# A hybrid decoder layer: TensorE's order from the recurrence to the second norm taken from a table, attention's half of the output projection first, latents left unscaled

## The chip, the cores and the metric

The kernel runs on one core of a Trainium2 chip. The metric is the device time of one execution in microseconds (us). A core has five engines with their own queues: TensorE (PE; its weight loads are PEld), VectorE (DVE), ScalarE (ACT), GpSimd (POOL) and SyncE (SP), which issues most DMAs. TensorE writes to PSUM, here eight banks of 128 x 512 floats; the other working memory is SBUF.

## The reference

One decoder layer on 256 tokens of width 2048, in float32:

```
h = rms_norm(x, attn_norm_g);  proj = h @ w_in
h_r, h_k, h_v, h_w, h_a, h_g = split(token_shift(proj[:, :3360]))
c_q, c_kv, k_pe = split(proj[:, 3360:])              # 512, 512, 64 columns
y_rwkv = (group_norm(rwkv7_scan(r, decay, k, v, -kk, kk * a)) + bonus) * g    # 16 heads x 64
q  = rms_norm(c_q)  @ w_uq;   kv = rms_norm(c_kv) @ w_ukv                     # the "latents"
y_mla = softmax((q_nope k_nope + rope(q_pe) rope(k_pe)) / sqrt(192)) v        # 8 heads, causal
x = x + concat(y_rwkv, y_mla) @ w_out
h = rms_norm(x, ffn_norm_g)                          # the second norm
x = x + (silu(conv3(h @ w_gate)) * (h @ w_up)) @ w_down
out = rms_norm(x, final_norm_g)
```

`rwkv7_scan` keeps a 64 x 64 state per head and updates it for every token: `state = state * w + (state a) b + v k`, output `state r`.

## The kernel before, in words

Every large weight comes as a *piece* of 128 x 1024 floats (512 KB). `piece` (L130) issues its DMA on SP's queue, casts it to a rounded `hi` on ScalarE (L138) and takes the rest `lo = raw - hi` on VectorE (L139). A product then is three matmuls: hi by hi, hi by lo, lo by hi. `raw`, `hi` and `lo` have three buffers each, so about three pieces can be ready ahead of TensorE. PSUM is divided into three banks `mm` (large products), three `ch` and two `at` (all small things).

The input projection runs tile by tile (`in_tile`, L226: two pieces, 48 matmuls). Keys come first, then receptance, then values. The recurrence is done in four chunks of 64 tokens and two halves of heads (`hf`). Its *factors* are built beside the projection: Gram matrices `G1`, the transposed `BKt`, and a triangular inverse. The inverse is found by `solve` (L612) on VectorE, 31 steps of two instructions, for 32 x 32 corners; the result goes through DRAM and comes back as `TT` and `T11` in another layout (L626 to L640). The remaining corners are 32 x 32 matmuls (`pR`, `pT`, L674 and L686), each followed by copies to `RT` and `TT`.

`chunk` (L705) is the recurrence: for each half a row product from local values and the state (`px`), the solved rows (`px` again, through `TT`), the output (`py`) from state and local values, and the state's update `ST`. Each is 8 small matmuls (16 instructions in the profile, L717), and each hands over to the next through VectorE or ScalarE copies (L743, L751, L760, L761, L767).

`latent` (L820) makes the two latents from input tiles 27 to 34: scaled by the first norm's `rsB` into `cr` (L826), squared and summed, split into `cl`, and their own root `rr` found on GpSimd by `rsqrt` (L233). `spread` (L858) turns `rr` into a row factor `rrB` by a matmul with ones (L262). `up_b` (L862) makes queries and keys (12 matmuls for each of two outputs) and multiplies each result by `rrB` on VectorE; L893 makes attention's values `vm`. `scores` (L906) and `attend` (L930) do one head. `group_norm` (L781) norms the recurrence's output for one half of the tokens, gates it (L803, L804) and transposes it into `yhi`/`ylo` (L808 to L812). The output projection (L968) has two halves: rows of the RWKV heads first, then rows of the attention heads. Behind the second, each 512-column tile of the new `x1` is transposed (L991) into `zs` for the feed-forward part, and the second norm's root is taken.

The order: the kernel is written in program order, and a scheduler that simulates a timeline orders each engine's instructions by readiness and program order. Before the change that also holds for TensorE in the stage that matters here; only `issue_after` binds some pairs. A block `manual_schedule(engines=...)` fixes the order in which an engine takes the instructions traced inside it.

## Time and profile before

| | |
|---|---|
| median of 3 runs (lowest to highest) | 1191.44 us (1190.81 to 1192.54) |
| the profiled execution | 1188.67 us |
| its span, first to last instruction | 1186.9 us |
| mean granted TensorE clock | 0.989 |
| TensorE busy | 1164.7 us (98%) |
| VectorE busy | 805.5 us (68%) |
| ScalarE busy | 603.9 us (51%) |
| bytes moved by DMA | 215.98 MB, mean 182 GB/s |

"Busy" is the union of instruction times. Matmuls are pipelined: one instruction's modelled end lies behind the start of the next, so the distance between starts tells what a matmul costs, and a busy TensorE can still be waiting or slow. The granted clock is 1.00 at full speed. A wait is idle time of an engine before an instruction, put down to what ended it. A row of the timeline begins with start and length in us, then engine, line, operation, result and operands, shapes and count.

### The profile page before, as it was taken

To read this page: it belongs to the slowest core of one execution; us is meant where nothing else is said; L and a number is where in the kernel's file an instruction comes from. 1 tells how busy PE (TensorE), PEld (TensorE's weight loads), DVE (VectorE), ACT (ScalarE), POOL (GpSimd) and SP (SyncE) were. 2 spreads that over 40 slices of the span, in tenths; PEclk is the share of its full clock that TensorE was granted. 3 is DMA by queue.
4 is the path that set the end of the run, shared out by engine and by line. 5 is a ranking of instruction groups with operands and counts; after the bars stand their busy time and mean duration, and the time that the engine had idled before them with its cause. 6 is when DMAs were issued, how large, how long until landed. Compare 5 with 4: busy or idle time off the path is not lost.

```text
span 1186.9 us, 19485 instructions
## 1 busy us (share of the span) xinstructions
PE 1164.7 (98%) x7673; PEld 1024.5 (86%) x7673; DVE 805.5 (68%) x1301; ACT 603.9 (51%) x894; POOL 29.4 (2%) x86
## 2 busy tenths in 40 slices
PE   9999999998989999999999999999999999999996
PEld 9899999997858888888888888888888888888885
DVE  7897669644975566777777775444577777775563
ACT  7874345433425456655555554333455555554441
POOL 1200000003000001000000000000000000000000
PEclk9999999998999999999999999999999999999998
DMA  9645456714425555656556566565555555566671
GB/s 335 196 148 162 134 169 195 220 53 127 160 89 171 161 184 176 197 194 195 193 184 194 192 195 192 193 190 192 195 194 194 195 189 189 194 228 212 199 227 71
DMA packets 71131, 215.98 MB, mean 182 GB/s; under 512 B 17616, under 2 KB 18000, under 8 KB 71040
## 3 DMA queue, kind: packets, MB, share of 16 engines
q1 hardware_dynamic: 69920, 211.97, 55.4%
q10 hardware_dynamic: 768, 2.05, 0.6%
q8 instruction: 60, 0.98, 0.3%
q0 software_dynamic: 352, 0.72, 0.2%
q14 instruction: 31, 0.25, 0.1%
HBM read 210.58 MB, written 3.41 MB: 180 GB/s over the span
## 4 chain that ended last, share of the span: by engine, by line
PE 92%; DVE 4%; DMA 1%; ACT 1%; issue 1%; POOL 1%; SPq 0%; ACTq 0%; DVEq 0%; POOLq 0%
PE mm L177 27%; PE mm L183 14%; PE mm L196 11%; PE mm L219 9%; PE mm L220 9%; PE mm L221 9%; PE mm L199 5%; PE pg L568 1%; PE px L717 1%; PE py L717 1%; DVE lo L139 1%; PE at L196 1%; PE wps L330 1%; DMA Lp<-dL 1%; DMA qs<-qr 0%
## 5 line engine op out<-in xcount | busy, mean ns | idle before, releaser
L139 DVE TENSOR_TENSOR lo<-raw,hi 128x1024 fp32r<-128x1024 f32 x376 | 460.0, 1224 | 269.7 <-ACT hi L138 202.7
L138 ACT CAST hi<-raw 128x1024 fp32r<-128x1024 f32 x376 | 395.5, 1053 | 421.5 <-PE mm L221 139.7
L177 PE MATMUL mm<-z,hi 128*128 128x512 f32 x1408 | 351.9, 392 | 0.0
L177 PEld LDWEIGHTS mm<-z,hi 128*128 128x128 f32 x1408 | 251.5, 188 | 43.0
L183 PEld LDWEIGHTS mm<-z,lo 128*128 128x128 f32 x1408 | 186.5, 188 | 14.9
L183 PE MATMUL mm<-z,lo 128*128 128x256 f32 x1408 | 189.3, 277 | 0.0
L196 PE MATMUL mm<-x,hi 128*128 128x256 f32 x1024 | 138.7, 284 | 0.0
L220 PE MATMUL mm<-lo,hh 128*128 128x512 f32 x336 | 130.7, 389 | 0.0
L221 PE MATMUL mm<-hi,hl 128*128 128x512 f32 x336 | 130.7, 389 | 0.0
L196 PEld LDWEIGHTS mm<-x,hi 128*128 128x128 f32 x1024 | 126.1, 190 | 2.1 <-issue 0.3
L219 PE MATMUL mm<-hi,hh 128*128 128x512 f32 x336 | 119.7, 389 | 0.0
L221 PEld LDWEIGHTS mm<-hi,hl 128*128 128x128 f32 x336 | 63.0, 188 | 13.2
L199 PE MATMUL mm<-x,lo 128*128 128x256 f32 x512 | 74.3, 283 | 0.0
L219 PEld LDWEIGHTS mm<-hi,hh 128*128 128x128 f32 x336 | 63.1, 188 | 13.0
L220 PEld LDWEIGHTS mm<-lo,hh 128*128 128x128 f32 x336 | 63.1, 188 | 13.0
L199 PEld LDWEIGHTS mm<-x,lo 128*128 128x128 f32 x512 | 65.8, 191 | 1.6 <-issue 1.3
L220 PE MATMUL mm<-lo,yhi 128*128 128x512 f32 x128 | 52.2, 408 | 0.0
L221 PE MATMUL mm<-hi,ylo 128*128 128x512 f32 x128 | 50.7, 397 | 0.0
L219 PE MATMUL mm<-hi,yhi 128*128 128x512 f32 x128 | 49.8, 406 | 0.3 <-ACT yhi L811 0.3
L219 PEld LDWEIGHTS mm<-hi,yhi 128*128 128x128 f32 x128 | 24.4, 192 | 7.1 <-issue 1.5
L196 PE MATMUL mm<-cl,hi 128*128 128x256 f32 x160 | 25.6, 306 | 4.8 <-DVE qr L209 2.0
L221 PEld LDWEIGHTS mm<-hi,ylo 128*128 128x128 f32 x128 | 24.5, 191 | 5.8 <-DVE bv L775 0.8
(279 smaller groups left out, 1057.1 us busy)
## 6 DMA issues: line engine op xcount, KB each, us to landing
raw<-in_wgu SPq DMA_DIRECT2D x176, 512.0 KB, 3.3
raw<-in_wdn SPq DMA_DIRECT2D x88, 512.0 KB, 4.2
raw<-in_win SPq DMA_DIRECT2D x70, 512.0 KB, 4.0
raw<-in_wout SPq DMA_DIRECT2D x32, 512.0 KB, 3.4
raw<-in_wuq SPq DMA_DIRECT2D x6, 512.0 KB, 4.4
xraw<-in_xT SPq DMA_DIRECT2D x4, 512.0 KB, 6.2
xt<-in_x SPq DMA_DIRECT2D x4, 512.0 KB, 6.8
raw<-in_wuv SPq DMA_DIRECT2D x4, 512.0 KB, 3.4
```

What stands on the lines that cost most here:

```text
L138: S.copy(hi, raw)
L139: last_lo[0] = V.tensor_tensor(lo, raw, hi.bitcast(F32), ALU.subtract).ins
L177: PE.matmul(accs[i], pcs[p][0][:, j * P:(j + 1) * P], act(h * 8 + j), start=h == 0 and j == 0, stop=False, skip_group_check=True)
L183: PE.matmul(accs[i][:, :T], lo[:, j * P:(j + 1) * P], act(h * 8 + j)[:, 0, :], start=False, stop=h == 1 and j == 7, skip_group_check=True)
L196: PE.matmul(acc[:, :T], hi[:, j * P:(j + 1) * P], act(kt0 + j)[:, s, :], start=first and j == 0 and s == 0, stop=False)
L199: i = PE.matmul(acc[:, :T], lo[:, j * P:(j + 1) * P], act(kt0 + j)[:, 0, :], start=False, stop=last and j == n - 1)
L219: PE.matmul(accs[tb], ah, wh, start=first and j == 0, stop=False)
L220: PE.matmul(accs[tb], ah, wl, start=False, stop=False)
L221: i = PE.matmul(accs[tb], al, wh, start=False, stop=last and j == n - 1)
L330: PE.matmul(wps[:, :P], ones, ones, start=True, stop=True)
L568: PE.matmul(pg[h][:, o:o + P], BK[pp][hs, gg, w * 2 + r, :, :], AR[pp][hs, gg, w * 2 + r, :, :], start=o == 0, stop=True, skip_group_check ...
L717: ins.append(PE.matmul(dst[HS[h], a_ * 64:(a_ + 1) * 64], lhsT, rhs, start=begin and n == 0 and a_ == 0, stop=True, skip_group_check=True) ...
```

## The change

From the corner matmuls to the transposes of `x1`, TensorE's instructions are written as short steps and put in one order by two strings, inside `manual_schedule(engines={PE})`. `STREAM` lists the large products (`l` latent tiles, `q` rope queries, `Q`/`K` queries and keys, `v` values, `W` output projection). They are generators that stop after 8 matmuls (256 columns) or 4 (512 columns): a latent tile has 6 steps, `q`, `Q`, `K` 3 each, `v` 6, `W` 12, 186 in all. `PLAN` is read from left to right: a number takes so many steps of the stream, a letter does one small unit.

- The latent tiles begin as before, while the solve runs; the corners `R` come after 32 steps, and most of chunks 0 to 2 between steps 34 and 38 of the stream.
- The latents are not multiplied by `rsB` any more: `cl` and the squares are taken straight from PSUM, and the first norm's root `rs1` (kept by one more GpSimd copy) enters the latents' roots, which now are taken on VectorE.
- Queries are not multiplied by `rrB` but copied by ScalarE; the factor `rrs[0]` goes into the maximum and the scale of the exponential. `spread` for the queries falls away. Keys and values are scaled as before.
- Heads are scored in the order 0, 2, 1, 3, 4, ..., with the transposes of the probabilities (`P`) and the products with the values (`A`) as separate units.
- The output projection takes attention's rows first (`W1..`), then the RWKV rows (`W0..`, tiles 0, 2, 1, 3). The group norms `N`, the gates `G` and the transposes `Y` lie beside the attention half. `x1` is transposed (`X`) near the end.
- The gate's loads wait for chunk 3's output copies instead of chunk 1's.

```
+        rs1 = con([P, 2], "rs1")
+        nc.gpsimd.tensor_copy(rs1, rsqrt(ssx[:, 0:2], 1.0 / DM, EPS, 2))
+        bcast(rs1, rsB)
...
+    def solved(c, hf):
+        pu = px_.pop((c, hf))[:, 256:512]
+        pairs(c, hf, pu, lambda p, a_, h: (TT[HS[h], c * 8 + p, :], XB[hf][HS[h], a_ * 64:(a_ + 1) * 64]), True)
+        for h in range(2):
+            (S.copy if h else V.tensor_copy)(UV[c][64:128, hf * 4:hf * 4 + 4, HS[h]],
+                                             pu[HS[h]].rearrange("p (a v) -> p a v", a=4))
...
+    def latent_tile(x, j):
...
+        h_, l_ = (c_[j // 2][:, j % 2, q, :] for q in range(2))
+        S.activation(h_, acc, AF.Copy, scale=vv(gname, j))
+        V.scalar_tensor_tensor(l_, acc, vv(gname, j), h_.bitcast(F32), ALU.mult, ALU.subtract)
+        sq = t2("csq") if j else ssum
+        S.activation(sq, acc, AF.Square)
+        if j:
+            V.tensor_tensor(ssum, ssum, sq, ALU.add)
...
+    def latent_root(x):
...
+        V.tensor_tensor(m, pss[:, 0:4:2], rs1, ALU.mult)
+        V.tensor_tensor(m, m, rs1, ALU.mult)
+        V.scalar_tensor_tensor(rrs[x], rsqrt(m, 1.0 / 512, EPS, 2, V), (SC, 1.0)[x], rs1, ALU.mult, ALU.mult)
...
+    def evict():
+        while waiting and (True and waiting[0][0] == 0 or waiting[0][0] in rrB):
+            x, dsts, accs = waiting.pop(0)
+            for j in range(2):
+                if True and x == 0:
+                    S.copy(dsts[j], accs[j][:, :T])
+                else:
+                    scaled(dsts[j], accs[j], rrB[x])
...
+    def gate_loads():
+        gnwb.extend([s4(n=n) for n in ("gnw", "gnb")])
+        with tc.issue_after(ylast[3]):
...
-            S.activation(pe_[:, ks], psc[:, ks], AF.Exp, bias=mx[:, qb:qb + 1], accum_out=sm[:, qb:qb + 1])
+            V.tensor_tensor(mx[:, qb:qb + 1], mx[:, qb:qb + 1], rrs[0][:, qb:qb + 1], ALU.mult)
+            S.activation(pe_[:, ks], psc[:, ks], AF.Exp, bias=mx[:, qb:qb + 1], scale=rrs[0][:, qb:qb + 1],
+                         accum_out=sm[:, qb:qb + 1])
...
+    small = {
+        "R": corner_r, "T": corner_t, "w": rows, "x": rows_state, "i": solved, "s": out_state, "u": update,
+        "o": out_local, "r": latent_root, "b": spread, "c": swap, "e": rope, "g": gate_loads, "S": scores,
+        "P": turn_p, "A": attend, "N": norm, "G": gated, "Y": turn_y, "X": turn_x,
+    }
+    STREAM = """
+    l00 l01 l02 l03 l10 l11 l12 l13 q0 q1 v0 K0 Q0 K1 Q1 v1 K2 Q2 Q3 K3 W100 W110 W120 W130 W001 W021
+    W011 W031
+    """.split()
+    PLAN = """
+    25 w00 3 r0 4 R0 R1 2 T0 w01 1 i00 i01 u00 w11 u01 w10 o01 T1 x10 x11 o00 s10 i10 i11 s11 u10 u11
+    w20 w21 o10 o11 x20 x21 s20 i20 i21 1 u20 s21 w30 1 u21 1 w31 o21 x31 x30 2 i31 1 s31 o20 1 o31 i30
+    g s30 3 o30 7 r1 5 c 3 b1 6 e 3 S0 3 S2 1 S1 1 P0 S3 1 P1 1 A0 4 P3 1 A1 3 N0 A3 1 P2 1 S4 1 S5 A2 3
+    S6 2 P4 1 P5 1 A5 2 A4 S7 1 P6 A6 2 P7 A7 4 N1 12 G00 1 G01 1 G10 Y01 16 G11 1 Y10 2 Y00 7 Y11 37
+    X10 1 X00 X01 X21 3 X11 1 X20 1 X30 X31
+    """.split()
+    with tc.manual_schedule(engines={mybir.EngineType.PE}):
+        big = stream()
+        for s in PLAN:
+            if s.isdigit():
+                for _ in range(int(s)):
+                    next(big, None)
+            else:
+                small[s[0]](*map(int, s[1:]))
+        for _ in big:
+            pass
```

## The prediction, made before the changed kernel was run

> **What bounds the kernel now.** The profile's page comes first: how long the profiled execution is, and what each weight piece costs VectorE.

> ```profile
> span 1186.9 us, 19485 instructions
> ...
> L139 DVE TENSOR_TENSOR lo<-raw,hi 128x1024 fp32r<-128x1024 f32 x376 | 460.0, 1224 | 269.7 <-ACT hi L138 202.7
> ```

> This execution took 1188.67 us (its span and 1.8 us around it); the three timed runs have a median of 1191.44 us. I sum against the profile and apply the difference to the median. The page says that TensorE is nearly always busy, but the change touches one stage, from the first latent tile to the second norm. So the second view is the table of stretches, cut at that stage's seams. Its columns are the length, busy time (instructions) of TensorE, its weight loads, VectorE, ScalarE and GpSimd, the granted TensorE clock, the DMA share and GB/s.

> ```profile
> core 0: us, PE busy (x) PEld busy (x) DVE busy (x) ACT busy (x) POOL busy (x), PEclk, DMA share, GB/s
> 194.20:228.60 34.40, 34.40 (x303) 34.28 (x301) 29.12 (x56) 18.40 (x27) 0.00 (x0) 1.00 0.71 206
> 231.90:235.20 3.30, 3.30 (x16) 3.30 (x17) 1.54 (x2) 1.89 (x3) 0.00 (x0) 0.50 0.97 374
> 254.70:261.40 6.70, 6.70 (x191) 6.25 (x190) 2.97 (x8) 1.89 (x6) 0.00 (x0) 1.00 0.23 81
> 276.40:279.70 3.30, 3.30 (x17) 3.30 (x17) 2.06 (x4) 1.76 (x3) 2.72 (x8) 0.51 0.40 92
> 283.50:290.10 6.60, 6.39 (x21) 5.59 (x22) 4.31 (x11) 1.04 (x1) 3.87 (x10) 0.52 0.53 130
> 290.10:346.30 56.20, 54.31 (x335) 45.19 (x333) 48.76 (x102) 22.97 (x40) 0.00 (x0) 1.00 0.46 145
> 351.30:358.10 6.80, 6.80 (x13) 3.40 (x12) 1.38 (x2) 1.15 (x2) 0.00 (x0) 0.50 0.00 0
> 358.10:453.20 95.10, 95.10 (x455) 78.81 (x454) 58.03 (x81) 48.29 (x83) 0.00 (x0) 1.00 0.55 177
> ```

> The reader is to see two things. From 358.1 on the projection has no idle time and a full clock, so nothing is to be gained there. Before it stand four stretches at about half the clock, 20 us in all: work in them takes twice as long although "busy" hides it. The list of waits of TensorE between 190 and 460 us names what stands ahead of most of them:

> ```profile
> PE pyT L808 <- DVE yt L805: 4.0, 1, 4.0
> PE mm L196 <- DVE qr L209: 2.0, 1, 2.0
> PE mm L196 <- DVE cr L209: 1.4, 1, 1.4
> PE mm L196 <- ACT vm L900: 1.3, 1, 1.3
> ```

> The first is the second group norm, which must be through before the output projection's first (RWKV) half can finish. The next two are the latents: their last tiles and their norms come after the recurrence, with nothing beside them. So TensorE is the bound, and it loses time where its order leaves it no independent work.

> **What the change takes away.** TensorE's work stays the same but for four small instructions of L262 (one broadcast less), so I count lost time, not work.

> (a) Latents beside the recurrence, not after it: waits of 2.0 and 1.4 us, and half the clock in 276.4–279.7 and 283.5–290.1, half of 9.9 us. That is 8.3 us.
> (b) L900's wait: `v0` is now followed by a small broadcast and a key tile; 1.3 us.
> (c) Attention's half of the projection first: the 4.0 us for L805, and half of 6.8 us of slow clock after it. 7.4 us. The cover is the attention half, four tiles that need no group norm.
> (d) The recurrence, interleaved finely with 256-column matmuls today. Its own rate and the fillers':

> ```profile
> 213.95 1.81 PE mm L196 x16
> 215.76 0.91 PE mm L199 x8
> 216.67 1.81 PE mm L196 x16
> ```

> ```profile
> 228.61 0.31 PE L674 MATMUL pR<-T,G 32*32 32x32 f32 x4
> ...
> 229.64 2.21 PE L674 MATMUL pR<-T,G 32*32 32x32 f32 x124
> ...
> 236.45 2.21 PE L686 MATMUL pT<-TT,RT 32*32 32x32 f32 x126
> ...
> 268.52 1.15 PE L717 MATMUL px<-ST,AR 64*64 64x64 f32 x32
> 269.51 1.10 PE L717 MATMUL py<-ST,AR 64*64 64x64 f32 x32
> ```

> Half a latent tile starts every 2.72 us; 32 recurrence instructions start every 0.99 us. Between 228.6 and 273.5 lie 21 groups of 32 (20.8 us), two corner bursts (4.4 us), 3.6 half tiles (9.8 us) and a 12-matmul up projection (1.4 us, an estimate at the same rate): 36.4 of 44.9 us. The slow stretch at 231.9 explains 1.6 us; 6.9 us are waits and switches. The table runs units of chunks 0 to 2 almost without filler, each with another unit between producer and consumer. I take 4.5 us as saved; bounds 0 (every handover waits as now) and 6.9.

> Taken away: 8.3 + 1.3 + 7.4 + 4.5 = 21.5 us; 22 with the broadcast, whose four instructions I put at 0.5 (the filler's 1.81/16 = 0.11 us each, for half as many columns in two passes).

> **What it adds.** (e) A fixed order holds everything behind a late operand. First place: `R0`, after 32 steps of eight matmuls (2.72/3 = 0.91 us each) and `w00`, about 30 us after the first latent tile. It needs T11, which comes from VectorE's solve through two DMA trips:

> ```profile
> 194.23 2.13 PE L196 MATMUL mm<-x,hi 128*128 128x256 f32 x16
> ```

> ```profile
> 224.14 2.60 SPq L636 DMA_DIRECT2D T<-dU  x2
> ```

> ```profile
> 200.39 0.42 DVE L209 TENSOR_TENSOR cr<-mm,rsB 128x256 f32<-128x256 f32 x1 [0.44 <-PE mm L199]
> ```

> Today T11's load is issued until 226.7 and the first corner matmul runs at 228.6, with latent tiles as filler. In the table `R0` is due at 194.2 + 30 = 224.2 to 224.5. VectorE loses four `cr` multiplications of 0.42 us ahead of the solve's end, so T11 comes up to 1.7 us sooner, at 226.9. TensorE waits 2.4 us, all later latent tiles behind it; bounds 0 (the solve gets more of VectorE) and 4.3 (it ends as now). (f) After an idle stretch and a low burst the clock drops once more: 1.7 us, half of 3.4; bounds 0 and 3.4.

> [...] At 283.5–290.1 TensorE was busy 6.39 of 6.60 us and the clock stayed at 0.52 throughout; after the 4.0 us wait it was 0.50 for 6.8 us. [...] I go by the rows.

> (g) Softmax, norms and splits share VectorE:

> ```profile
> 280.00:358.00 78.00, 15.34 (x24) 0.91 0.42 132
> ```

> ```profile
> 280.00:358.00 78.00, 9.87 (x10) 0.91 0.42 132
> ```

> ```profile
> L922 DVE TENSOR_REDUCE mx<-psc 128x1 f32<-128x128 f32 (+1 forms) x9 | 3.0, 344 | 0.0
> ...
> L879 DVE TENSOR_TENSOR qr<-qr,cosR 128x1024 f32<-128x1024 f32 x1 | 1.2, 1228 | 6.3 <-DMA qs<-qr 6.3
> ```

> The first two rows are VectorE's time on `yt` and on `bv` in the two group norms, about 12.6 us a norm. VectorE is 87% busy in 290.1–346.3, and TensorE lost 1.9 us there. The change takes 12 query multiplications of 0.42 (5 us) off it. It adds 16 small multiplications before the exponentials and the two roots (about 14 small operations each, from GpSimd): 44 operations, at the 0.20 us of GpSimd's own row below some 9 us, at most. Both sums meet an engine near full, now under an order that can't give way. `N0` stands ahead of four heads' softmax. I take 3.5 us; bounds 0 and 8. (h) Rope: three passes of 1.23 us after the swap's DMAs, emitted three steps (2.7 us) before `S0` needs them: 1.2 us; bounds 0 and 5, if the DMAs (6.3 us waited for today) outlast the nine steps between swap and rope. (i) Tile boundaries of the projection, with three PSUM buffers, and `X30`, `X31` right behind the last tile: 0.7 us; bounds 0 and 2, since today's row at 358.1 shows none. (j) `rs1`, one more GpSimd operation before the first norm is spread:

> ```profile
> 35.42 0.20 POOL L253 TENSOR_TENSOR ry<-ry,rt 128x2 f32<-128x2 f32 x1
> ```

> 0.3 us with its handover; bounds 0 and 0.6.

> At nothing: the gate's loads, issued behind chunk 3's copies instead of chunk 1's (ScalarE's later copies queue behind four issues), are read 70 steps later; latents taken straight from PSUM hold their bank through three readers, but the third bank gives 5 us; query evictions move to ScalarE, 41% busy in 290.1–346.3. Without those covers each costs one handover, within (g)'s bound.

> Added: 2.4 + 1.7 + 3.5 + 1.2 + 0.7 + 0.3 = 9.8 us. Net 22.0 − 9.8 = 12.2 us saved: 1191.44 − 12.2 = 1179.2. With my best values the forecast is 1179.

> **Rivals.** *Nearly all handovers meet.* (e), (g), (h) vanish and (d) is whole: 9.5 us more, about 1170. For it: units alternate, and `S` to `P` have several steps between. Against: `R0`'s arithmetic.

> *The clock stays low in the recurrence.* Some 14 us of 64-column work with one filler step follow `R0`'s wait. If the half clock holds, it costs up to 14 us, or 7 when half of the issue is not bound by the clock: 1186. Against: 254.7–261.4 is such work at 1.00; but it came from a full clock.

> *The waits only move.* `R0` at its bound (+1.9), two slow stretches (+1.7), rope at its bound (+3.8), (d) not saved (+4.5): 11.9 back, 1191, no change.

> *Slower: VectorE serves the norms before the splits.* `N0`, `N1` are emitted ahead of the later weight pieces. If 12.6 us of norm run before the next split, TensorE has two prepared pieces of 2.7 us, waits 7 us, and then runs 6.8 us at half clock: 10.5 per norm, 21 in place of (g)'s 3.5. That is 17.5 back on 12.2 saved: 1197. It decides from the point at which more than 5.4 us of norm stand before a split. Against: in 290.1–346.3 norm operations alternate with splits and TensorE lost little.

> **Numbers.** Forecast 0.46 (its own range 1174 to 1184); nearly all meets 0.18; low clock 0.14; waits move 0.09; slower 0.13. 0.2% is 2.4 us, about what a measurement of this kernel can tell from no change. Faster: the first three but for the low clock's dear end, and a third of the fourth, 0.80; same 0.07; slower 0.13. The range of 8 in 10 runs from 1168 (below "nearly all") to 1191 (through "waits move"); it leaves out the slower rival and tails.

> **What would show it.** Right: no wait of TensorE on L805's successor or on a latent's norm; full clock from the corners' end to the projection's; the stage from first latent tile to last projection matmul 247 us instead of 259 (194.2 to 453.2); a wait of some 2 us on T11 before the first corner burst. Wrong: half clock across the recurrence (second rival), waits of a `mm` matmul on `lo` while VectorE works on `yt` (slower), several waits over 3 us on `S0` and the corners (third).

## The result, and the profile after

The changed kernel takes 1184.77 us (median of 7 runs, 1181.36 to 1187.61) against 1190.81 us for the kernel before on the same chip (7 runs, 1188.55 to 1192.87): a ratio of 0.9948, 95% interval 0.9930 to 0.9966. It saves 6.0 us, half of the 12.2 that were forecast. The profiled execution took 1185.31 us, its span is 1183.5 us, the mean granted clock 0.995. The two profiled executions lie only 3.4 us apart: the one before the change took 2.1 us less than this median, the one after it 0.5 us more.

First the table of stretches of the kernel after, cut at the seams of the same stage.

```profile
core 0: us, PE busy (x) PEld busy (x) DVE busy (x) ACT busy (x) POOL busy (x), PEclk, DMA share, GB/s
194.80:228.50 33.70, 31.37 (x283) 30.89 (x281) 28.36 (x65) 16.52 (x25) 0.00 (x0) 1.00 0.67 197
228.50:235.30 6.80, 6.76 (x141) 6.70 (x142) 2.53 (x3) 1.15 (x2) 0.00 (x0) 0.52 0.70 192
235.30:273.50 38.20, 37.98 (x882) 34.99 (x881) 16.93 (x33) 18.08 (x40) 0.00 (x0) 1.00 0.25 79
273.50:310.00 36.50, 35.11 (x247) 32.32 (x245) 27.56 (x62) 18.15 (x36) 1.97 (x4) 1.00 0.62 184
310.00:356.00 46.00, 44.04 (x262) 37.98 (x262) 42.02 (x105) 26.30 (x56) 0.00 (x0) 1.00 0.38 127
356.00:443.80 87.80, 86.48 (x378) 66.47 (x378) 52.16 (x62) 38.38 (x54) 0.00 (x0) 1.00 0.53 173
```

One stretch at half clock is left of four, 6.8 us behind the first corner. The list of TensorE's waits of the kernel after (from 150 to 460 us; total, count, longest) says what stands ahead of it, and what else is left:

```profile
PE pR L676 <- DMA T<-dU: 2.4, 2, 1.8
PE po L975 <- ACT pT L969: 1.8, 2, 1.2
PE mm L896 <- ACT qn L886: 1.4, 2, 0.9
PE mm L177 <- DVE z L1042: 1.0, 1, 1.0
```

The four waits quoted before the change (4.0, 2.0, 1.4 and 1.3 us) are gone. The stage from the first latent tile to the start of the last projection matmul takes 248.9 us (194.8 to 443.7) in place of 258.7 (194.2 to 452.9); 247 was forecast.

So the saving was there when the feed-forward began. The four matmuls that spread the second norm's root show it, first in the kernel before, then after; the times are those of the first and last of the four:

```profile
L262 PE MATMUL rsb<-dg,ones x4: 272/275/275, 464.7 to 465.0; 128*128 128x128 f32 x4
```

```profile
L262 PE MATMUL rsb<-dg,ones x4: 270/274/275, 455.3 to 455.6; 128*128 128x128 f32 x4
```

Here 9.4 us are saved, but at the end of the span only 3.4. The change touches no line behind this point, and TensorE waits for nothing there in either kernel. Yet in the same 220 us, all busy and at full clock, it gets through 17 instructions fewer. The table of stretches, before and then after:

```profile
480.00:700.00 220.00, 220.00 (x1285) 193.56 (x1285) 161.17 (x243) 124.47 (x181) 0.00 (x0) 1.00 0.59 192
```

```profile
480.00:700.00 220.00, 220.00 (x1268) 192.52 (x1267) 158.47 (x239) 122.32 (x177) 0.00 (x0) 1.00 0.58 190
```

The groups of instructions say which. Columns: line, operation, result and operands, shapes, count, then busy time in us and the mean of one in ns. Before:

```profile
L177 PE MATMUL mm<-z,hi 128*128 128x512 f32 x1408 | 351.9, 392 | 0.0
L183 PE MATMUL mm<-z,lo 128*128 128x256 f32 x1408 | 189.3, 277 | 0.0
L220 PE MATMUL mm<-lo,hh 128*128 128x512 f32 x336 | 130.7, 389 | 0.0
```

After:

```profile
L177 PE MATMUL mm<-z,hi 128*128 128x512 f32 x1408 | 355.2, 393 | 1.0 <-DVE z L1042 1.0
L183 PE MATMUL mm<-z,lo 128*128 128x256 f32 x1408 | 192.6, 279 | 0.0
L220 PE MATMUL mm<-lo,hh 128*128 128x512 f32 x336 | 130.7, 389 | 0.0
```

The matmuls that read `z`, the second norm's output, are slower by 3.3 us in each group; the down projection is not. The mean of one hardly shows it: at 277 and 279 ns it is more than twice the distance between starts. The timeline shows it: eight L183 matmuls in a row, before and after.

```profile
607.83 1.07 PE L183 MATMUL mm<-z,lo 128*128 128x256 f32 x8
```

```profile
600.33 1.11 PE L183 MATMUL mm<-z,lo 128*128 128x256 f32 x8
```

Less the last one's 0.28 us, seven distances take 0.79 and 0.83 us: 113 and 118 ns. Before the change 150 of the 175 undivided runs of eight have about the first value, after it two in three have the second. Over all 1408 the mean distance is 114.0 ns before and 116.4 after; of L177's, 229.0 and 231.1. 1408 times 2.4 and 2.1 ns are 6.3 us.

Why, if neither line nor order changed there? A difference lies in the allocation. (Places are in bytes of a partition, modulo 256; they come from the allocator, not from a trace. The expectations call 256 bytes a line: the runs move tiles by 32 and by 128 bytes, so the 256 is the author's unit, and no run measures it.) `z` has four tiles. Each takes the slot of an older one, with a 128-byte offset on every other tile, so that in the kernel before all four began at 32. In the changed kernel the keys' tile is allocated ahead of the queries', these two swap slots, and `z` inherits that: its first two tiles now begin at 160, the others at 32. A second difference: `rs1` moves all that is allocated behind it by 32 bytes.

### The profile page after: what moved, and what is told of

Read it like the earlier page. It is cut to its first block, busy times and chain, and to the rows that moved or that the text cites. A ratio compares the mean times of both kernels' runs of the same rounds, so it can differ in the third digit from the quotient of the medians.

```text
span 1183.5 us, 19464 instructions
## 1 busy us (share of the span) xinstructions
PE 1164.0 (98%) x7669; PEld 1022.3 (86%) x7669; DVE 803.8 (68%) x1318; ACT 608.6 (51%) x906; POOL 22.0 (2%) x59
## 3 DMA queue, kind: packets, MB, share of 16 engines
HBM read 210.58 MB, written 3.41 MB: 181 GB/s over the span
## 4 chain that ended last, share of the span: by engine, by line
PE 91%; DMA 3%; DVE 3%; ACT 2%; issue 0%; SPq 0%; ACTq 0%; DVEq 0%
PE mm L177 28%; PE mm L183 14%; PE mm L837 8%; PE mm L221 7%; PE mm L220 7%; PE mm L219 7%; PE mm L196 6%; PE mm L822 3%; PE mm L199 3%; PE mm L896 2%; DMA raw<-in_win 1%; PE pg L570 1%; DVE lo L139 1%; ACT hi L138 1%; PE py L714 1%; PE px L714 1%
## 5 line engine op out<-in xcount | busy, mean ns | idle before, releaser
L139 DVE TENSOR_TENSOR lo<-raw,hi 128x1024 fp32r<-128x1024 f32 x376 | 459.7, 1223 | 274.7 <-ACT hi L138 201.5
L138 ACT CAST hi<-raw 128x1024 fp32r<-128x1024 f32 x376 | 395.1, 1052 | 428.4 <-PE mm L177 137.6
L177 PE MATMUL mm<-z,hi 128*128 128x512 f32 x1408 | 355.2, 393 | 1.0 <-DVE z L1042 1.0
L177 PEld LDWEIGHTS mm<-z,hi 128*128 128x128 f32 x1408 | 251.6, 188 | 47.3 <-DVE z L1042 1.2
L183 PEld LDWEIGHTS mm<-z,lo 128*128 128x128 f32 x1408 | 189.2, 188 | 14.8
L183 PE MATMUL mm<-z,lo 128*128 128x256 f32 x1408 | 192.6, 279 | 0.0
L196 PE MATMUL mm<-x,hi 128*128 128x256 f32 x768 | 102.9, 282 | 0.0
L196 PEld LDWEIGHTS mm<-x,hi 128*128 128x128 f32 x768 | 93.7, 188 | 1.6 <-issue 0.3
L199 PE MATMUL mm<-x,lo 128*128 128x256 f32 x384 | 55.2, 281 | 0.0
L199 PEld LDWEIGHTS mm<-x,lo 128*128 128x128 f32 x384 | 48.7, 188 | 1.4 <-issue 1.3
L822 PE MATMUL mm<-x,hi 128*128 128x256 f32 x256 | 34.5, 285 | 0.0
L822 PEld LDWEIGHTS mm<-x,hi 128*128 128x128 f32 x256 | 31.8, 193 | 0.5
L837 PEld LDWEIGHTS mm<-lo,yhi 128*128 128x128 f32 x128 | 24.1, 188 | 6.2 <-issue 1.5
```

Of the source, the lines that this page charges most:

```text
L138: S.copy(hi, raw)
L139: last_lo[0] = V.tensor_tensor(lo, raw, hi.bitcast(F32), ALU.subtract).ins
L177: PE.matmul(accs[i], pcs[p][0][:, j * P:(j + 1) * P], act(h * 8 + j), start=h == 0 and j == 0, stop=False, skip_group_check=True)
L183: PE.matmul(accs[i][:, :T], lo[:, j * P:(j + 1) * P], act(h * 8 + j)[:, 0, :], start=False, stop=h == 1 and j == 7, skip_group_check=True)
L196: PE.matmul(acc[:, :T], hi[:, j * P:(j + 1) * P], act(kt0 + j)[:, s, :], start=first and j == 0 and s == 0, stop=False)
L199: i = PE.matmul(acc[:, :T], lo[:, j * P:(j + 1) * P], act(kt0 + j)[:, 0, :], start=False, stop=last and j == n - 1)
```

## Experiments: where the six microseconds went

Three theories: the place of `z` (P), the 32-byte shift (S), or the moment at which weight pieces arrive and are split (T).

**z put back.** One line ahead of the stream.

```
+        buf("qn")
         big = stream()
```

> The changed kernel with the queries' tile allocated ahead of the keys' tile, as the kernel before had it; the only effect is that the first two of the four z tiles lie in each other's place again (byte 16544 and byte 41504 of a partition, with the 128-byte offset on the first of them). Theory P (place of z): the feed-forward's matmuls that read z collide with something because z's first two tiles changed places; then the mean distance from one L183 matmul to the next goes back from 116.3 to 113.5 ns, the 6.2 us that were lost after the second norm come back, and the time is 1184.8 - 6.2 = 1178.6 us. Theory S (shift): the 32 bytes of rs1 are at fault; then nothing changes, 116.3 ns and 1184.8 us. Theory T (turn): neither place matters; what matters is the moment at which weight pieces arrive and are split beside the matmuls; then 116.3 ns and 1184.8 us as well, or any value between if the moment happens to move.

Measured: 1178.90 us, ratio 0.9891 (0.9877 to 0.9905). The distance is 114.0 ns again. P holds, and T falls: up to the second norm's root (455.3 us in both) the two executions run alike, and only the place of `z` differs.

```profile
L177 PE MATMUL mm<-z,hi 128*128 128x512 f32 x1408 | 352.3, 392 | 1.0 <-DVE z L1042 1.0
L183 PE MATMUL mm<-z,lo 128*128 128x256 f32 x1408 | 189.2, 276 | 0.0
```

**The shift undone.**

```
-        rs1 = con([P, 2], "rs1")
+        rs1 = pad2[:, 0:2]
```

> The changed kernel with rs1 kept in two columns of a pad that is there already, so that no later tile of the pool is moved by 32 bytes against the kernel before; z's first two tiles stay in their changed places. Theory S (shift): L183's distance goes back from 116.3 to 113.5 ns and the time to 1178.6 us. Theory P (place of z) and theory T (turn): nothing changes, 116.3 ns and 1184.8 us within 1 us.

Measured: 1182.19 us, ratio 0.9928 (0.9915 to 0.9941), and 116.4 ns as in the changed kernel. S falls. The 2.6 us below the changed kernel's median are not in the feed-forward; in this profile T11 came earlier (0.8 us of wait in place of 2.4) and no half-clock stretch followed.

**The kernel before with the two slots swapped.**

```
-    qn, kn = a8("qn", F32), a8("kn", F32)
+    kn, qn = a8("kn", F32), a8("qn", F32)
```

> The kernel before with the keys' tile allocated ahead of the queries' tile, so that the first two z tiles change places as they do in the changed kernel; nothing else is touched. Theory P (place of z): the feed-forward slows by 6.2 us, L183's distance goes from 113.5 to 116.3 ns, and the time is 1190.8 + 6.2 = 1197.0 us. Theories S (shift) and T (turn): 113.5 ns and 1190.8 us.

Measured: 1198.45 us, ratio 1.0055 (1.0042 to 1.0067); the distance goes to 116.3 ns. The same loss, without any of the change.

```profile
L177 PE MATMUL mm<-z,hi 128*128 128x512 f32 x1408 | 354.8, 393 | 0.0
L183 PE MATMUL mm<-z,lo 128*128 128x256 f32 x1408 | 192.6, 279 | 0.0
```

**Which property of the place?** Slots left swapped, the offset chosen anew: all four tiles at 32, then all at 160.

```
-            zs.extend(hl4("z", 1) for _ in range(4))
+            zs.extend(hl4("z", int(q > 1)) for q in range(4))      # all at 32
```

```
+            zs.extend(hl4("z", int(q < 2)) for q in range(4))      # all at 160
```

> The changed kernel, z's first two tiles in their changed places, but the 128-byte offset given to the second of them and not to the first, so that all four z tiles begin 32 bytes into a 256-byte line again, as in the kernel before (in the changed kernel two begin at 32 and two at 160). Theory L (line): what matters is where in a 256-byte line z begins; then L183's distance is 113.5 ns and the time 1178.9 us, as with the tiles put back. Theory A (absolute place): what matters is which tile of z lies where in the partition; then 116.3 ns and 1184.8 us stay.

> The changed kernel with the offset of z's last two tiles turned round, so that all four z tiles begin 160 bytes into a 256-byte line. Theory L1 (only a mixture is bad): L183's distance 113.5 ns and 1178.9 us. Theory L2 (160 is the bad place, 32 the good one, and half of the tiles are now in it): the loss doubles, about 119 ns and 1184.8 + 5.9 = 1190.7 us. Theory A (absolute place): 116.3 ns and 1184.8 us.

Measured: 1177.45 us, ratio 0.9886 (0.9871 to 0.9900), and 114.0 ns; 1185.57 us, ratio 0.9956 (0.9943 to 0.9970), with 115.4 ns for L183 and 232.8 for L177. So the slot is indifferent, and the 128 bytes by which a tile was moved count (theory L). Of these two places 160 is the bad one, so a mixture is not what hurts (L1), but the loss did not double as L2 said either: from the second norm to the last matmul on `z` it is 603.5 us at 32, 609.8 with both, 610.7 at 160.

**Is it z's own place, or its place against the weights?** On the kernel with all of `z` at 160. `raw`, `hi` and `lo` begin at 224. With 128 bytes of padding ahead of them they begin at 96, and `z` at 160 lies to them as 32 to 224.

```
     def piece(src, dst=None):
+        if last_w[0] is None:
+            nc.gpsimd.memset(con([P, 32], "pad3"), 0.0)
```

> The kernel with all z tiles 160 bytes into a line (1185.6 us), with 128 bytes of padding ahead of the weight buffers (raw, hi and lo), so that these begin 96 in place of 224 bytes into a line and z lies to them as it does in the kernel before (32 and 224); everything that is allocated after them moves by 128 bytes as well. Theory R (relation): what matters is where z lies against the weight buffers or another of the tiles moved; then L183's distance is 113.5 ns and the time 1185.6 - 7.3 = 1178.3 us. Theory O (own place): z's own place in the line matters; then about 116 ns and 1185.6 us.

Measured: 1186.87 us, ratio 0.9960 (0.9946 to 0.9974). The time says "own place", the profile says otherwise (line numbers are two higher here):

```profile
L179 PE MATMUL mm<-z,hi 128*128 128x512 f32 x1408 | 352.3, 392 | 1.0 <-DVE z L1044 1.0
L185 PE MATMUL mm<-z,lo 128*128 128x256 f32 x1408 | 189.3, 277 | 0.0
L222 PE MATMUL mm<-lo,hh 128*128 128x512 f32 x336 | 133.1, 396 | 0.0
```

The `z` matmuls are fast again though `z` did not move, so a relation counts (R). That its other side is the weight buffers is likely but not shown: everything allocated behind the padding moved with them. What was gained there was lost elsewhere: the down projection went from 389 to 396 ns (6.7 us over its two blocks), and the mean distance of matmuls that read `x` from 115.2 to 117.7 ns (1680 of them, 4.2 us).

## Experiments: the clock, the corner and the two other parts

**R0 four steps later.** `8 R0` in place of `4 R0`, and `3 r1` in place of `7 r1`.

> The changed kernel with the R corner's first burst four steps of the stream later (8 in place of 4 steps between the first root and R0), and the same four steps fewer between the last recurrence output and the second root, so that attention keeps its place in the stream. By the prediction's term (e) the 2.4 us wait for the DMA of the T11 block is gone, and the two half-clock windows stay: 1184.8 - 2.4 = 1182.4 us. Rival: the half-clock windows come with an idle stretch of TensorE, and without the wait one of them goes too: 2.4 + 1.7 less, 1180.7 us. Rival: the four steps are missed after the recurrence, where the first group norm or the second root is then waited for: 1184.8 us or more.

Measured: 1184.13 us, ratio 0.9932 (0.9920 to 0.9944), not separable from the changed kernel. The wait for T11 is gone, and TensorE waits 2.4 us before T0 instead. Rows of this run's timeline (idle time before, and what ended it, in brackets):

```profile
224.84 2.34 SPq L642 DMA_DIRECT2D TT<-dT  x3
...
227.22 1.03 SPq L132 DMA_DIRECT2D raw<-in_win  x2
...
229.34 2.21 PE L676 MATMUL pR<-T,G 32*32 32x32 f32 x128
...
232.31 1.06 ACT L138 CAST hi<-raw 128x1024 fp32r<-128x1024 f32 x1 [5.54 <-DMA raw<-in_win]
233.40 1.23 DVE L139 TENSOR_TENSOR lo<-raw,hi 128x1024 fp32r<-128x1024 f32 x1 [5.37 <-ACT hi L138]
234.66 1.28 DVE L680 COPY RT<-pR 32x512 f32<-32x512 f32 x2
235.37 1.18 ACT L680 COPY RT<-pR 32x512 f32<-32x512 f32 x2 [2.01 <-DVE RT L680]
236.00 1.20 PE L689 MATMUL pT<-TT,RT 32*32 32x32 f32 x64 [2.42 <-ACT RT L680]
```

The corner is through at 231.5, but its copies stand on ScalarE and VectorE behind the cast and split of a weight piece. That piece's load stood on SP's queue behind the loads of the T blocks, which wait there for their stores (in the changed kernel SP's queue waits 3.1 us for the store to `dT`). T0 starts at 236.0; in the changed kernel it starts at 235.7. The table fixes TensorE's order, but the other engines' queues were made late too.

**The T blocks' loads taken off SP's queue.** On the kernel with `z` put back and R0 four steps later, L638 and L642 are issued by `nc.gpsimd` in place of `nc.sync`.

> The repaired kernel (the changed kernel with z's tiles put back, 1178.9 us), with R0 four steps later, and with the six loads of the T blocks that SyncE issues (L638, L642), two of which wait there for the stores before them, issued by GpSimd; no raw weight piece waits behind them on SyncE. Theory Q (the queue): with R0 four steps later T0 ran at 235.8 us all the same, because the casts of ScalarE ahead of the corner's copies waited for weight pieces whose loads stood behind the T loads on SyncE; now R0 finds T11 there, T0 runs 4 us earlier, TensorE has no idle stretch over 1 us before the recurrence and no half-clock window there: 1178.9 - 2.4 - 3.4 = 1173.1 us. Rival: T11 itself comes later through GpSimd's queue, R0 waits again and the clock halves again: 1178.9 us or more. Rival: the weight pieces wait for something else (their buffers), so that T0 stays at 235.8 us: 1177.2 us (one half-clock window fewer).

Measured: 1184.76 us, ratio 0.9954 (0.9941 to 0.9967). The first rival: R0 waits 7.4 us. The rows of DMA issues (KB each, median us from issue to landing), with SP's queue (`z` put back, R0 in its old place) and then with GpSimd's:

```profile
T<-dU SPq DMA_DIRECT2D x2, 128.0 KB, 4.5
```

```profile
T<-dU POOLq DMA_DIRECT2D x2, 128.0 KB, 11.9
```

GpSimd also issued them late, from 225.2 us on, behind the four loads of `TT`. Whether the loads would have gained in a third queue is left open.

**R0 one step later.** On the kernel with all of `z` at 32: `5 R0` and `6 r1`.

> The kernel with all z tiles 32 bytes into a line (1177.5 us), with R0 one step of the stream later (5 in place of 4 after the first root) and one step fewer before the second root. Theory I (idle): the clock halves after an idle stretch of TensorE of more than about 1 us (idle 1.8 and 0.6 us ahead of R0 gave two windows, 0.6 and 0.3 us gave none); the step of 0.9 us is taken out of the 2.2 us wait, and what is left is near that edge: 1177.5 - 0.9 - 1.7 = 1174.9 us if the window goes, 1176.6 us if it stays. Theory W (low bursts): 32-row matmuls halve the clock whatever stands before them: 1176.6 us, and a window in the profile. Rival: T0 waits 0.9 us more in R0's stead, as with four steps: 1177.5 us.

Measured: 1175.77 us, ratio 0.9868 (0.9850 to 0.9886), the lowest of all kernels here; against the same without the step (0.9886) the intervals overlap. The wait fell to 1.4 us, and one half-clock window stayed.

**x at 32 too.** `hl4("x", 1)` in place of `hl4("x")`, on the kernel of the experiment above.

> The kernel with all z tiles 32 bytes into a line and R0 one step later, and the four x tiles too moved from 160 to 32 bytes into a line. In the profile so far 620 of the 1680 matmuls that read x start 117 to 119 ns after the one before, the others 113 or 114. Theory L (line, for every moving operand): these go to 113.5 ns as well and 620 x 4.5 ns = 2.8 us fall away where TensorE bounds: 1174.9 - 2.8 = 1172.1 us. Rival: the line matters for z alone, because of what runs beside the feed-forward: 1174.9 us. Rival: the x stage is bounded by its loads and splits: 1174.9 us with the shorter distance.

Measured: 1176.78 us, ratio 0.9880 (0.9861 to 0.9898). The expectation fell: nearly all `x` matmuls now start 117 to 119 ns apart (mean 117.6; 115.4 without the edit). That is 3.7 us more. It was hidden: the later stream found T11 there, so 1.4 us of wait and a half-clock window (1.7 us) went. For `x` the bad place is where for `z` the good one is.

**Latents scaled again.** On the kernel with `z` put back.

```
+        cr = t2("cr")
+        scaled(cr, acc, rsB)
+        acc = cr
...
-        V.tensor_tensor(m, pss[:, 0:4:2], rs1, ALU.mult)
-        V.tensor_tensor(m, m, rs1, ALU.mult)
-        V.scalar_tensor_tensor(rrs[x], rsqrt(m, 1.0 / 512, EPS, 2, V), (SC, 1.0)[x], rs1, ALU.mult, ALU.mult)
+        V.tensor_copy(m, pss[:, 0:4:2])
+        V.tensor_scalar(rrs[x], rsqrt(m, 1.0 / 512, EPS, 2, V), (SC, 1.0)[x], None, ALU.mult)
```

> The repaired kernel (1178.9 us) with the third part of the change undone: each latent tile is first multiplied by the first norm's row factor on VectorE, as in the kernel before (eight more multiplications of 0.42 us, 3.4 us of VectorE), and the roots leave the factor out. Theory of the prediction's term (e): VectorE's solve comes up to 1.7 us later (the four multiplications ahead of its end), TensorE's wait for T11 grows from 2.4 to about 4.1 us, and the rest of the multiplications is hidden: 1180.6 us. Rival: the multiplications stand in chains that TensorE waits for (the second root, the up projections): up to 3.4 us, 1182.3 us. Rival: all hidden, 1178.9 us.

Measured: 1182.29 us, ratio 0.9931 (0.9919 to 0.9943): 3.4 us more than without the edit. The wait of R0 is 4.4 us in place of 2.0, and four half-clock windows follow in place of two. The end of the solve on VectorE shows why, with unscaled latents (here the changed kernel; with `z` put back the same copy starts at 217.31) and then with scaled ones:

```profile
216.92 1.14 DVE L631 COPY tp<-Tq 128x1024 f32<-128x1024 f32 x1
```

```profile
216.90 0.21 DVE L625 TENSOR_TENSOR tm<-Tq,Lp 128x31 f32<-128x31 f32 x1
217.22 0.42 DVE L209 TENSOR_TENSOR cr<-mm,rsB 128x256 f32<-128x256 f32 x1
217.56 1.22 DVE L139 TENSOR_TENSOR lo<-raw,hi 128x1024 fp32r<-128x1024 f32 x1
218.69 0.21 DVE L627 TENSOR_TENSOR Tq<-Tq,tm 128x31 f32<-128x31 f32 x1
...
219.87 1.13 DVE L631 COPY tp<-Tq 128x1024 f32<-128x1024 f32 x1
```

So unscaled latents pay by the solve, which ends 2.6 us sooner than with the same kernel scaled. The four multiplications of 0.42 us alone don't make this: in the scaled kernel one of them and a weight split stand between the two halves of the solve's last step, and three further small operations (`cl`, `css`, `XB`) before its copy, where the other kernel has nothing. No run separates the share of the changed order from that of the multiplications themselves.

**The RWKV half first.** On the kernel with all of `z` at 32; the norms, gates and turns move ahead in the table.

```
-    ... W100 W110 W120 W130 W001 W021 W011 W031
+    ... W000 W010 W020 W030 W101 W121 W111 W131
...
+    ... S0 3 S2 N0 1 S1 1 P0 S3 1 P1 1 A0 4 P3 1 A1 N1 3 A3 1 P2 G00 1 S4 G10 1 S5 A2 Y00 1 Y10 2
+    G01 G11 Y01 S6 2 Y11 P4 1 P5 1 A5 2 A4 S7 1 P6 A6 2 P7 A7 81
```

> The kernel with all z tiles 32 bytes into a line (1177.5 us), with the second part of the change undone in the table: the projection's RWKV half comes first and attention's half second; for that the group norms stand in the middle of the attention heads (N0 after S2, N1 after A1) and the gates and turns (G, Y) before the projection. By the prediction's term (c) the second norm is late again and the clock halves behind it: 1177.5 + 7.4 = 1184.9 us. Rival: a table can put the norms early enough, TensorE waits for nothing more, and the order of the halves is worth nothing by itself: 1177.5 us. Rival: VectorE works on the norms while softmax and the weight splits wait: more than 1184.9 us.

Measured: 1189.98 us, ratio 0.9989 (0.9978 to 1.0000): 12.5 us more than with attention's half first. The waits of TensorE and the stretch in which they lie:

```profile
PE ptp L968 <- DVE pexp L960: 5.4, 1, 5.4
PE mm L896 <- DVE kn L209: 2.6, 1, 2.6
```

```profile
280.00:303.00 23.00, 18.98 (x118) 17.05 (x117) 21.46 (x34) 8.45 (x11) 1.97 (x4) 0.93 0.49 146
303.00:326.00 23.00, 17.63 (x95) 15.09 (x94) 20.14 (x64) 12.11 (x30) 0.00 (x0) 0.85 0.24 83
```

VectorE is 90% busy there: softmax and the keys wait behind the norms (and the rope), and the clock halves twice. So by this table the order of the halves is worth more than the 7.4 us of term (c). The norms moved ahead with it, so this is not (c) alone, and a better table for this order was not looked for.

**Idle time and half clock, over the twelve kernels ordered by the table.** In the changed kernel eight L822 matmuls took 2.08 us at half clock (231.97) and 1.10 at full (222.96), so a half-clock window of 3.4 us is put at 1.7 us lost. The first corner waits differently long in each kernel. The windows behind it, read from stretches of 0.5 us:

| wait before the first corner, us | windows of 3.4 us |
|---|---|
| 7.4; 4.4 | 3; 4 |
| 2.4; 2.1; 2.0 | 2; 2; 2 |
| 2.2; 2.0; 1.4 | 1; 1; 1 |
| 0.8; 0.6 | 0; 1 |
| 0 (x at 32) | 0 |
| 0 at R0, 2.4 before T0 (R0 four steps later) | 1, behind T0 |

The burst of 32-row matmuls is the same in all of them. From 1.4 us of wait on there was always at least one window. But idle time is not needed: the kernel before had a window right behind the same burst (its stretch at 231.9 us) with no wait ahead of it.

The table becomes less puzzling when the trace is cut where its clock changes. Within each trace all changes lie whole multiples of 3.41 us apart (in the kernel before, windows begin at 231.87, 276.24, 283.07 and 351.33 us). Where this grid lies differs between executions, so the same wait falls into one interval or is split over two. In the stage of all fourteen traces, each interval in which TensorE was idle for 1.9 us or more was followed by one at half clock; from 1.6 to 1.8 us some were and some not (in the kernel before 1.71 us at 272.83 was, 1.68 at 344.51 was not). Less was followed by a window in some intervals that held 32-row matmuls (0 us in the kernel before, 0.9 us with R0 one step later), in some that were at half clock themselves (0.6 us at 283.07 in the kernel before), and in one that was neither (some 1.0 us at 273.9 with the two slots swapped in the kernel before). No run moves the grid on purpose, so what decides below 1.9 us stays open.

## Why the prediction was right in sign and half in size

**The step that failed first** is the first sentence of the sum: "TensorE's work stays the same but for four small instructions of L262 (one broadcast less), so I count lost time, not work." The instructions stayed the same, but 2816 of them became longer by 2.1 or 2.4 ns: 6.3 us. No term of the prediction had a place for it. With `z` put back, the time is 1178.90 us; the forecast was 1179. That this fits so well is partly luck. The sum was made from a profiled execution of 1188.67 us, and against that one the kernel with `z` put back saves 9.8 us, not 12.2. The terms in the stage fell short, and the 2.8 us between that execution and the median, which no run explains, filled the gap.

**(a), (b), (c)** are shown: the four waits are gone, and of their slow stretches none is left. Undoing the order of the halves costs 12.5 us, more than (c).

**(d)** is the second step that failed. The stage became 9.8 us shorter. Its listed waits fell from 9.7 to 7.1 us. Its half-clock stretches fell from 20.0 to 6.8 us, which is 6.6 us of lost time at half speed. Together these are 9.2 us, so 0.6 us is left for (d) and the broadcast, forecast at 5.0. The 6.9 us that (d) called "waits and switches" held no waits: from 228.6 to 273.4 us the kernel before has none in its list. The step went wrong at the rate. The sum took 0.99 us for 32 recurrence instructions from one clean row, 31 ns each; on average the 672 of them started 36 ns apart before the change, which is some 3.5 of the 6.9 us, and 35 ns after it.

**(e)** 2.4 us forecast, 2.4 measured. The mechanism behind it is shown by the scaled latents: VectorE's solve sets T11. The size is luck in part: TensorE was through with the steps ahead of `R0` at 225.9 us and not at 224.2 to 224.5, and the corner could go on at 227.7 and 228.5 us and not at 226.9. In the six other kernels with `R0` at this step and unscaled latents the wait was 0.6 to 2.2 us.

**(f)** One window more was forecast than the kernel before had behind its corner, 1.7 us; in the profile two stand there in place of one. In the six kernels just named it was none, one or two. With R0 one step later one followed 1.4 us of wait, in the kernel before one came with no wait ahead of it, and with the scaled latents there were four, with TensorE busy 4.00 of 4.00 us in the last ones (235 to 239 and 239 to 243).

**(g)** 3.5 forecast, 3.2 measured in its place, but by another mechanism, so the size is luck: the list names ScalarE's copies (`pT`, `qn`) and not VectorE. In the longer wait of each kind the copy starts when ScalarE is through with the cast of a weight piece. The query copies are among what the prediction put at nothing; they cost 1.4 us. **(h)** 1.2 forecast, no wait before `S0`. **(i)** 0.7 forecast, about 1.3 measured, 1.0 of it for another reason (`z`, read by a feed-forward matmul that the scheduler put among the last projection tiles). **(j)** the stage begins 0.6 us later in this execution (0.3 forecast); between two single executions this is no proof.

**The rivals.** Low clock in the recurrence: 1.00 from 235.3 to 273.5, refuted here; with the 4.4 us wait of the scaled latents the half clock did reach 3.5 us into the recurrence. Waits only move: no; R0's is the only one of its list. Slower by VectorE: not here, because the norms lie beside attention's half of the projection; with the RWKV half first its mechanism came, VectorE serving norms while TensorE waits.

## What to carry to other kernels

When an edit moves time in a stage that it does not touch, compare the starts of the same instructions there, then where their operands lie: a changed order of allocation can cost what the changed order of work gained. Before time is called waiting, look for the wait in the list, and take a rate from the average of the stretch and not from its cleanest row. A wait in front of a tuned stretch is priced with the half-clock windows that follow it, here 1.7 us for each. And an order fixed for one engine moves the other engines' queues too: TensorE's wait for T11 came back as a wait for copies stuck behind a weight piece.
